# Eight of twelve w_down block sums moved from the projections to the input unit stage, and the down stage's operand loads queued in order of use

## The chip, the cores and the metric

The kernel runs on one NeuronCore of one Trainium2 chip, in one launch. The metric is the device time in microseconds (us); smaller is better. Engines: PE (TensorE, matrix products), DVE (VectorE), ACT (ScalarE), POOL (GpSimd) and SP (SyncE, which here only issues DMA loads). Every engine runs its own instructions in a fixed order; semaphores tie the engines together.

## The reference

One layer of a diffusion backbone over 1024 latent tokens of width 1024, with 256 context tokens. All data are float32.

```python
hx = rmsnorm(x, g_pre_mix) * (1 + sc1) + sh1                # sc, sh, ga: silu(c) @ w_mod + b_mod
u_pool, u_lru, u_gate, g_pool, g_lru = split(hx @ w_in)     # 5 x 1024 columns
y_pool = pool_mixer(u_pool)                                 # window sums, then 4 small products
y_lru  = (h_f + h_b) * gelu(u_gate)                         # two linear scans of gated u_lru
m = sigmoid(g_pool) * (y_pool @ w_proj_pool) + sigmoid(g_lru) * (y_lru @ w_proj_lru)
x = x + ga1 * rmsnorm(m @ w_out)
g, u = split(modulated_rmsnorm(x) @ w_up)                   # 2 x 3072 columns
g = depthwise_conv3x3(g) + b                                # on a 16 x 64 grid
x = x + ga2 * rmsnorm((gelu(g) * u) @ w_down)               # w_down is 3072 x 1024
```

## The kernel before, in words

Each float32 product is made of three products of a rounded high part and a low remainder. `split` makes the two: ACT casts the high part (line 89), DVE subtracts (line 90). `load_w` (lines 92 to 99) loads 512 KB of weights into one of three buffers with the tag "raw" and splits them into one of three "whl" buffers, from which PE multiplies.

The stages, with their place in the span:

- **Preparation** (0 to 80 us): the modulation vectors that the input needs, and normalised tokens hx.
- **Input units** (80 to 280, the pool `z1`): the list `steps` (line 403) names what the program does one after another. `p`, `u`, `g` are units: one `load_w` of w_in and 48 matrix instructions of 128x512 (`unit_mm`, line 243). `a` and `b` are the products after the pooling (`pw`, line 378, stored to yp_d), `c` and `t` prepare the context tokens, and each `m` takes three steps of the generator `mod_steps` (lines 253 to 282).
- **mod_steps** makes two modulation vectors here (j = 0 and 1). For each it loads eight blocks of w_mod (`rawm`) one after another and adds them into `acc` on DVE (lines 265 and 267), sums over the partitions on PE (`pm`, line 271), adds a row of rowv (`rowb`, line 274) and stores the row (line 281). `rawm` and `rowb` use the same three "raw" buffers as `load_w`.
- **LRU** (280 to 590, the pool `z2`): `lru_in(0)` (line 450) begins with a `load_w` of w_in, and its `unit_mm` is the first work of PE in the stage.
- **Projections** (590 to 820, the pool `pj`): first yps, the last gate units and hy; then eight `pp_unit` and eight `pl_unit` (48 matrix instructions each; a pl unit ends with two operations on DVE, lines 603 and 604, and a store of a block of m_d). Among them stand twelve `down_sums` (line 616) and three `form_pair`, and the loads of w_out (`wo`).
- **Output projection** (827 to 940): for each of eight row blocks a load of `st` from m_d, a split into `mH` (lines 718 and 719) and matrix instructions of line 724.
- **Feed-forward** (945 to 1413): 24 features f; the last act of each is a convolution of eight taps on DVE (line 881), a gelu on ACT (line 889), a product on DVE (line 890) and a store to gu_d.
- **Down stage** (1400 to the end): seven products of twelve sets each. `down_set` loads two halves of a set into a ring of three "raw" and five "rw" buffers (lines 908 and 910) and splits it into three "whl" and five "op" buffers; line 971 multiplies. Sets 0 to 2 of the first product are prepared ahead (line 927), set 3 is the first in an "rw" buffer.

A call of `down_sums(p)` loads the blocks p and 12+p of w_down (512 KB each, on SP), makes four additions of 128x512 on DVE (lines 620 to 623) and stores two blocks of 512 KB to sd_d (on POOL's queue). Four of the seven products of the down stage read sd_d, from the third on. In the kernel before these blocks lie in tiles `pc` of the projection pool.

The order of each engine's instructions is set by a scheduler from the program order and priorities; a DMA on SP waits for its buffer to be free, and the DMAs behind it on SP wait as well.

Of the kernel before, what the change touches and what calls it, by code (L numbers as in the profile page):

```python
# [8 lines left out]
F32 = mybir.dt.float32  # L9
# [31 lines left out]
def block_kernel(ctx: ExitStack, tc: tile.TileContext, x, cx, vecs, rowv, icnt, w_mod1, w_mod, w_in, pool_w,  # L41
# [50 lines left out]
    def load_w(src, n=1024, tag="whl", bufs=3, pool=None, raw=None):  # L92
        if raw is None:
            raw = gpool.tile([P, n], F32, name=uid("raw"), tag="raw", bufs=3)
        nc.sync.dma_start(raw, src)
        w = (pool or gpool).tile([P, 2, n], F32R, name=uid("whl"), tag=tag, bufs=bufs)
        with tc.high_priority(offset=WPRI):
            split(w[:, 0, :], w[:, 1, :], raw)
        return w

    n2raw = gpool.tile([P, 4, 512], F32, name="n2raw", tag="n2raw")
    epsc = cpool.tile([P, 1], F32, name="epsc")
# [185 lines left out]
    with tc.tile_pool(name="z1", bufs=1, reuse_waits="tile") as zp:  # L288
# [111 lines left out]
                modulate(hc[0][:, k, :], hc[1][:, k, :], xcT[:, k, :], k, 1)  # L400

        NHO = 2
        steps = "p6 p7 u6 g6 u7 p4 g7 a3 p5 b3 u4 u5 c m t m p2 a2 u2 p3 b2 m u3 m p0 a1 p1 b1 u0 m u1 m a0 b0".split()
        base = {"p": 0, "u": 16, "g": 24}
        order = [base[s_[0]] + int(s_[1:]) for s_ in steps if s_[0] in base]
        wq = pre
# [2 lines left out]
        for s_ in steps:  # L409
            kind, n = s_[0], int(s_[1:] or 0)  # L410
            if kind in base:
                while n_ld < len(order) and len(wq) < 3:
                    wq.append(load_w(w_in[order[n_ld]]))
                    n_ld += 1
            if kind == "p":
                mm = pool_unit(n)
            elif kind == "u":
                mm = ug_unit(n)
            elif kind == "g":
                mm = gate_unit(0, n)  # L420
            elif kind in "ab":
                pool_out(n, "ab".index(kind), mm)
            elif kind == "c":
                ctx_norm()
            elif kind == "t":
                ctx_mod(mm)
            else:
                some(mods, 3)
# [126 lines left out]
    with tc.tile_pool(name="pj", bufs=1, reuse_waits="tile") as zp:  # L555
# [54 lines left out]
        def piece(dt=F32R):  # L610
            n_pc[0] += 1
            i = n_pc[0] % 5
            return zp.tile([P, 2, 512], dt, name=uid("pc"), tag="mq" if i < 2 else f"bc{i - 2}",
                           bufs=NMQ if i < 2 else 1)

        def down_sums(p):
            ru, rg = piece(F32), piece(F32)
            nc.sync.dma_start(ru, w_down[p * P:(p + 1) * P, :].rearrange("p (h c) -> p h c", h=2))
            nc.sync.dma_start(rg, w_down[(NH + p) * P:(NH + p + 1) * P, :].rearrange("p (h c) -> p h c", h=2))
            V.tensor_add(rg[:, 1, :], ru[:, 1, :], rg[:, 1, :])  # L620
            V.tensor_add(ru[:, 1, :], ru[:, 0, :], ru[:, 1, :])
            V.tensor_add(ru[:, 0, :], ru[:, 0, :], rg[:, 1, :])
            V.tensor_add(rg[:, 0, :], rg[:, 0, :], ru[:, 0, :])
            for i, t in enumerate((ru, rg)):
                G.dma_start(sd_d[p, i], t.rearrange("p h c -> p (h c)"))

        def form_pair(f):
            L, R = slice(0, 512), slice(512, 1024)
            ru, rg = [gpool.tile([P, 1024], F32, name=uid("raw"), tag="raw", bufs=3) for _ in range(2)]
# [17 lines left out]
        wo = []  # L647
        for c in range(4):
            pp_unit(c)
            down_sums(c)  # L650
        for c in range(KT):
            m_last = pl_unit(c)
            if c < 2:
                down_sums(4 + c)
            elif c < 2 + NPF:
                form_pair(c - 2)
            else:
                for p in range(2):
                    down_sums(6 + 2 * (c - 2 - NPF) + p)
            if c < 4:  # L660
                pp_unit(c + 4)
            if c >= 4 and c < 6:
                for k in range(4 * c - 16, 4 * c - 12):
                    wo.append(load_w(w_out[k * P:(k + 1) * P, :], tag="big", bufs=8, pool=zp))
# [106 lines left out]
    with tc.tile_pool(name="ff", bufs=1, reuse_waits="tile") as zp:  # L771
# [131 lines left out]
            ("Y", False, lambda p: wlo(1)(p)[:, H1], gul(1, 0), "n4"),  # L903
        ]

        def down_set(q, p, raw, op, raw2=None):
            dst, first, wsrc, gsrc, form = PRODS[q]
            nc.sync.dma_start(raw[:, H0], wsrc(p))
            if gsrc is not None:
                nc.sync.dma_start(raw[:, H1], gsrc(p))  # L910
            if form == "n2":
                nc.sync.dma_start(raw2[:, H0], gul(0, 1)(p))
                nc.sync.dma_start(raw2[:, H1], gul(1, 1)(p))
            with tc.high_priority(offset=DPRI):
                if form == "n2":
                    V.tensor_sub(N[:, 0, p, :], raw[:, H1], raw2[:, H0])
                    V.scalar_tensor_tensor(N[:, 1, p, :], raw2[:, H1], -1.0, N[:, 0, p, :],
                                           op0=ALU.mult, op1=ALU.subtract)
                elif form in ("n3", "n4"):
                    V.tensor_add(raw[:, H1], raw[:, H1], N[:, 1, p, :])  # L920
                if form in ("n1", "n2"):
                    split(op[:, 0, H0], op[:, 1, H0], raw[:, H0])
                    split(op[:, 0, H1], op[:, 1, H1], N[:, int(form[1]) - 1, p, :])
                else:
                    split(op[:, 0, :], op[:, 1, :], raw)
            return op
# [189 lines left out]
```

## Time and profile before

| | |
|---|---|
| median of 3 runs | 1656.9 us (1655.75 to 1661.22) |
| the profiled execution's own time | 1658.86 us |
| its span | 1657.1 us |
| PE busy | 1568.0 us, 95% |
| DVE busy | 1244.5 us, 75% |
| ACT busy | 684.1 us, 41% |
| POOL busy | 163.3 us, 10% |
| DMA | 267.12 MB, mean 161 GB/s |

Times of rows are microseconds from the start of the span. Busy time is time in instructions; a row of an engine in order of time gives in brackets how long the engine was idle before the instruction and what released it. PEclk is the clock that TensorE was granted, as a share of full speed. "To landing" is the time from the issue of a DMA to its completion.

### The profile page before, as it was taken

The page shows a single profiled execution, that of the slowest core. Times are in us where ns is not written, and L with a number is a line of the kernel's source. Part 1 is how long each engine was busy: PE and PEld are TensorE (multiplying, and loading weights), DVE is VectorE, ACT ScalarE, POOL GpSimd, SP SyncE. Part 2 cuts the span into 40 slices and gives each one's busy share as a digit, 9 for nine tenths or more (in the row PEclk, how much of TensorE's full clock was granted, in tenths as well). Part 3 has the DMA queues.
Part 4 walks back from the last instruction along what each step waited for, and adds up shares of the span by engine and source line. Part 5 has one row for each costly group of instructions (what it writes and reads, how often), then busy time and mean ns, then how long its engine had stood idle before and what let it go on. Part 6 is the DMA issues. An engine that isn't in the chain of part 4 may idle for free.

```text
span 1657.1 us, 18358 instructions
## 1 busy us (share of the span) xinstructions
PE 1568.0 (95%) x6976; PEld 1267.1 (76%) x6976; DVE 1244.5 (75%) x1416; ACT 684.1 (41%) x828; POOL 163.3 (10%) x232
## 2 busy tenths in 40 slices
PE   6899999999899999998699889999999999799997
PEld 4588888877778788886488667888888888588886
DVE  7777574787887745565457879999999998677567
ACT  8523322655577643122034333333433333445443
POOL 1300200111112221121110000000000000000000
PEclk9999999999999999999899999999999999899999
DMA  8335354324232277899934432222222222885544
GB/s 311 114 100 172 127 196 141 121 83 152 77 127 89 89 261 286 294 326 339 344 114 165 166 114 76 88 78 78 88 86 80 76 89 102 276 296 201 191 166 165
DMA packets 87990, 267.12 MB, mean 161 GB/s; under 512 B 9719, under 2 KB 9847, under 8 KB 87134
## 3 DMA queue, kind: packets, MB, share of 16 engines
q1 hardware_dynamic: 64382, 183.23, 33.2%
q0 software_dynamic: 23520, 82.73, 13.3%
q8 instruction: 54, 0.88, 0.2%
q14 instruction: 34, 0.28, 0.1%
HBM read 199.32 MB, written 66.60 MB: 160 GB/s over the span
## 4 chain that ended last, share of the span: by engine, by line
PE 29%; DVE 15%; DMA 3%; ACT 2%; issue 1%; DVEq 0%; ACTq 0%
PE pb L971 7%; DVE gc L881 6%; PE pb L724 5%; PE pb L758 5%; PE pd L971 4%; PE pc L971 3%; DMA raw<-in_w_up_dram 3%; PE pc L758 3%; PE pd L758 2%; DVE wf L90 2%; DVE gc L890 1%; DVE whl L90 1%; ACT whl L89 1%; DVE gc L865 1%; DVE raw L811 1%
## 5 line engine op out<-in xcount | busy, mean ns | idle before, releaser
L243 PE MATMUL pu<-hx,whl 128*128 128x512 f32 x1056 | 266.7, 392 | 1.5 <-DVE whl L90 1.3
L881 DVE SCALAR_TENSOR_TENSOR gc<-gc,vec 128x945 f32<-128x945 f32 (+1 forms) x192 | 234.4, 1221 | 7.1 <-ACT gc L870 2.9
L89 ACT CAST whl<-raw 128x1024 fp32r<-128x1024 f32 (+1 forms) x109 | 108.9, 1001 | 294.1 <-PE pu L243 58.8
L243 PEld LDWEIGHTS pu<-hx,whl 128*128 128x128 f32 x1056 | 186.7, 188 | 39.6 <-DVE whl L90 2.0
L90 DVE TENSOR_TENSOR whl<-raw,whl 128x1024 fp32r<-128x1024 f32 (+1 forms) x109 | 127.9, 1178 | 88.7 <-ACT whl L89 88.4
L243 PE MATMUL pg<-hx,whl 128*128 128x512 f32 x480 | 116.0, 394 | 0.0
L243 PEld LDWEIGHTS pg<-hx,whl 128*128 128x128 f32 x480 | 88.9, 189 | 19.1
L243 PE MATMUL pb<-hy,whl 128*128 128x512 f32 x384 | 93.1, 403 | 10.3 <-DVE sgp L603 5.9
L724 PE MATMUL pb<-whl,mH 128*128 128x512 f32 x384 | 91.0, 398 | 11.4 <-ACT mH L718 11.4
L243 PEld LDWEIGHTS pb<-hy,whl 128*128 128x128 f32 x384 | 74.4, 195 | 28.2 <-ACT whl L89 8.0
L758 PE MATMUL pb<-h,wf 128*128 128x512 f32 x384 | 93.0, 391 | 2.1 <-ACT fk L820 2.1
L758 PE MATMUL pb<-h,whl 128*128 128x512 f32 x384 | 94.5, 390 | 0.0
L724 PEld LDWEIGHTS pb<-whl,mH 128*128 128x128 f32 x384 | 73.2, 192 | 27.2 <-ACT mH L718 11.8
L89 ACT CAST wf<-raw 128x1024 fp32r<-128x1024 f32 x42 | 44.2, 1052 | 118.4 <-PE pb L758 53.1
L758 PEld LDWEIGHTS pb<-h,wf 128*128 128x128 f32 x384 | 71.5, 188 | 18.8 <-ACT fk L820 4.2
L758 PEld LDWEIGHTS pb<-h,whl 128*128 128x128 f32 x384 | 71.9, 188 | 15.3 <-ACT fk L820 0.5
L758 PE MATMUL pc<-nf,wf 128*128 128x512 f32 x288 | 73.7, 404 | 8.7 <-ACT nf L778 4.5
L971 PE MATMUL pb<-op 128*128 128x512 f32 x306 | 79.0, 394 | 0.0
L758 PEld LDWEIGHTS pc<-nf,wf 128*128 128x128 f32 x288 | 53.7, 192 | 26.6 <-DVE gc L865 7.6
L499 PE MATMUL pg<-xp,whl 128*128 128x512 f32 x192 | 62.2, 420 | 8.9 <-ACT i L505 8.5
L758 PE MATMUL pc<-nf,w 128*128 128x512 f32 x288 | 69.2, 389 | 0.0
L971 PEld LDWEIGHTS pb<-op 128*128 128x128 f32 x306 | 58.2, 191 | 12.5 <-DVE CA L999 0.3
(310 smaller groups left out, 2952.1 us busy)
## 6 DMA issues: line engine op xcount, KB each, us to landing
raw<-in_w_up_dram SPq DMA_DIRECT2D x51, 512.0 KB, 3.6
raw<-in_w_in_dram SPq DMA_DIRECT2D x40, 512.0 KB, 4.7
rawm<-in_w_mod_dram SPq DMA_DIRECT2D x32, 512.0 KB, 4.1
rw<-gu_d SPq DMA_DIRECT2D x63, 256.0 KB, 4.4
pc<-in_w_down_dram SPq DMA_DIRECT2D x24, 512.0 KB, 5.9
sd_d<-pc POOLq DMA_DIRECT2D x24, 512.0 KB, 6.3
gu_d<-gc POOLq DMA_DIRECT2D x24, 512.0 KB, 2.9
raw<-gu_d SPq DMA_DIRECT2D x33, 256.0 KB, 3.3
```

What stands on the lines that cost most here:

```text
L89: A.copy(hi, src)
L90: V.tensor_sub(lo, src, f32(hi))
L243: mm = T.matmul(ps[:, h * 512:(h + 1) * 512], wv[:, wi, k, :], act(h, k, ai), start=st, stop=sp)
L499: T.matmul(pg[:, h * 512:(h + 1) * 512], wg[:, wi, m, :], xp[:, ai, h * 512:(h + 1) * 512], start=(i == 0), stop=(i == 2))
L724: mm = T.matmul(ps[:, h * 512:(h + 1) * 512], mh[ai][:, k, :], wo[k][:, wi, h * 512:(h + 1) * 512], start=(k == 0 and i == 0), stop=(k == ...
L758: mm = T.matmul(ps, w(wi, j), b(ai, j), start=(start and j == 0 and i == 0), stop=(j == 3 and i == 2), skip_group_check=True)
L811: V.tensor_add(ru[:, L], ru[:, L], rg[:, R])
L865: V.tensor_sub(gc[:, 0, 0:512], v, u2)
L881: V.scalar_tensor_tensor(o, gv[:, r0 + dr:r1 + dr, c0 + dc:c1 + dc], cw(i, j), o, op0=ALU.mult, op1=ALU.add)
L890: V.tensor_mul(gc[:, 1, :], gc[:, 0, :], u)
L971: T.matmul(bank[dst](t), op[:, gi, 512 + t * P:512 + (t + 1) * P], op[:, wi, H0], start=(first and p == 0 and i == 0), stop=(p == NH - 1 a ...
```

## The change

Three things change in the program:

1. `down_sums` becomes a helper that is given its two tiles. Eight of its twelve calls (p = 0 to 7) become the steps `d0` to `d7` of the input unit stage, with two tiles of the tag "raw" each, so they share the three buffers of `load_w` and `mod_steps`.
2. In the projections only four calls (p = 8 to 11, after pp_unit 0 to 3) stay; those after the pl units are gone.
3. Each load of `down_set` is ordered behind the load of the set before it (`issue_after`).

```diff
+    def down_sums(p, tiles):
+        ru, rg = [t if len(t.shape) == 3 else t.rearrange("p (h c) -> p h c", h=2) for t in tiles]
+        nc.sync.dma_start(ru, w_down[p * P:(p + 1) * P, :].rearrange("p (h c) -> p h c", h=2))
...
-        steps = "p6 p7 u6 g6 u7 p4 g7 a3 p5 b3 u4 u5 c m t m p2 a2 u2 p3 b2 m u3 m p0 a1 p1 b1 u0 m u1 m a0 b0".split()
+        steps = "p6 p7 u6 g6 u7 p4 g7 a3 p5 b3 u4 d0 u5 d1 c m t m p2 a2 u2 d2 p3 b2 m u3 d3 m p0 a1 d4 p1 b1 u0 d5 m u1 d6 m a0 b0 d7".split()
...
+            elif kind == "d":
+                down_sums(n, [gpool.tile([P, D], F32, name=uid("raw"), tag="raw", bufs=3) for _ in range(2)])
...
             pp_unit(c)
-            down_sums(c)
+            down_sums(NH - 4 + c, (piece(F32), piece(F32)))
         for c in range(KT):
             m_last = pl_unit(c)
-            if c < 2:
-                down_sums(4 + c)
-            elif c < 2 + NPF:
+            if 2 <= c < 2 + NPF:
                 form_pair(c - 2)
-            else:
-                for p in range(2):
-                    down_sums(6 + 2 * (c - 2 - NPF) + p)
...
+        ld = []
+
         def down_set(q, p, raw, op, raw2=None):
             dst, first, wsrc, gsrc, form = PRODS[q]
-            nc.sync.dma_start(raw[:, H0], wsrc(p))
...
+            with ExitStack() as es:
+                if ld:
+                    es.enter_context(tc.issue_after(ld[-1].ins))
+                ld.append(nc.sync.dma_start(raw[:, H0], wsrc(p)))
+                if gsrc is not None:
+                    ld.append(nc.sync.dma_start(raw[:, H1], gsrc(p)))
```

Line numbers after the change are higher by 11 to 13 in the stages before the projections (line 262 becomes 273, line 271 becomes 282), and by 2 in the down stage.

**SP at the end of the input unit stage.** These are the last loads of the stage, up to the weights of `lru_in(0)` (the last row but one before, the last after). Before:

```order
L262 DMA rawm235_1943<-in_w_mod_dram 128x1024
L262 DMA rawm238_1998<-in_w_mod_dram 128x1024
L262 DMA rawm239_2001<-in_w_mod_dram 128x1024
L256 DMA rowb241_2007<-in_rowv_dram 1x1024
L95 DMA raw254_2078<-in_w_in_dram 128x1024
L95 DMA raw256_2083<-in_lru_w_dram 128x512
```

After:

```order
L273 DMA rawm247_2003<-in_w_mod_dram 128x1024
L103 DMA raw250_2058<-in_w_down_dram 128x1024
L104 DMA raw251_2059<-in_w_down_dram 128x1024
L273 DMA rawm252_2068<-in_w_mod_dram 128x1024
L273 DMA rawm253_2071<-in_w_mod_dram 128x1024
L267 DMA rowb255_2077<-in_rowv_dram 1x1024
L103 DMA raw262_2117<-in_w_down_dram 128x1024
L104 DMA raw263_2118<-in_w_down_dram 128x1024
L95 DMA raw270_2158<-in_w_in_dram 128x1024
```

The loads of the sums d6 (raw250, raw251) and d7 (raw262, raw263) now stand among and behind the last blocks of w_mod and ahead of the weights of `lru_in(0)` (raw270). raw270 takes the buffer of rowb255 and waits until DVE has read that row at line 285.

**DVE at the same place.** The end of the second modulation vector (`acc`), the last pooling outputs (`yp`), and the remainder of the weights of `lru_in(0)`. Before:

```order
L90 TENSOR_TENSOR whl255_2080<-raw254_2078,whl255_2080 128x1024
L342 TENSOR_TENSOR q225_1857<-up224_1854 128x16x64
L384 TENSOR_SCALAR yp228_1867<-pw230_1876,vec_67 128x512
L90 TENSOR_TENSOR pw214_1769<-praw213_1767,pw214_1769 128x512
L90 TENSOR_TENSOR d217_1779<-xa216_1774,d217_1779 128x1024
L349 TENSOR_TENSOR xa226_1859<-q225_1857 128x1024
L351 TENSOR_TENSOR xa226_1859<-xa226_1859,inv212_1765 128x1024
L352 TENSOR_TENSOR xa226_1859<-xa226_1859,up224_1854 128x1024
L90 TENSOR_TENSOR d227_1864<-xa226_1859,d227_1864 128x1024
L274 TENSOR_TENSOR acc204_1698<-pm240_2004,rowb241_2007 1x1024
L384 TENSOR_SCALAR yp242_2011<-pw244_2020,vec_67 128x512
```

After:

```order
L278 SCALAR_TENSOR_TENSOR acc212_1738<-rawm252_2068,cs_89,acc212_1738 128x1024
L395 TENSOR_SCALAR yp256_2081<-pw258_2090,vec_67 128x512
L278 SCALAR_TENSOR_TENSOR acc212_1738<-rawm253_2071,cs_89,acc212_1738 128x1024
L395 TENSOR_SCALAR yp259_2099<-pw261_2108,vec_67 128x512
L285 TENSOR_TENSOR acc212_1738<-pm254_2074,rowb255_2077 1x1024
L105 TENSOR_TENSOR raw263_2118<-raw262_2117,raw263_2118 128x512
L106 TENSOR_TENSOR raw262_2117<-raw262_2117 128x512
L107 TENSOR_TENSOR raw262_2117<-raw262_2117,raw263_2118 128x512
L108 TENSOR_TENSOR raw263_2118<-raw263_2118,raw262_2117 128x512
L90 TENSOR_TENSOR whl271_2160<-raw270_2158,whl271_2160 128x1024
```

Before, the weights of `lru_in(0)` (whl255) were split nine operations ahead of the addition of `pm`. Now that addition stands behind the last pooling outputs, and the weights (whl271) are split after it. On PE the two instructions of `pm` stand directly before the first of `lru_in(0)`; before, the 24 of the last pooling product stood between.

**SP at the start of the down stage.** Sets 0 to 2 are in raw1016 to raw1020; the set 3 is rw1022, the first one that is loaded into an "rw" buffer. Before:

```order
L910 DMA raw1020_9415<-gu_d_6509 128x512
L908 DMA raw1032_9558<-in_w_down_dram 128x512
L910 DMA raw1032_9558<-gu_d_6509 128x512
L908 DMA raw1034_9576<-in_w_down_dram 128x512
...
L908 DMA raw1052_9742<-in_w_down_dram 128x512
L910 DMA raw1052_9742<-gu_d_6509 128x512
L908 DMA rw1022_9426<-in_w_down_dram 128x512
```

After:

```order
L912 DMA raw1020_9415<-gu_d_6509 128x512
L910 DMA rw1022_9426<-in_w_down_dram 128x512
L912 DMA rw1022_9426<-gu_d_6509 128x512
L982 DMA ga_9435<-row_d_82 128x1024
L910 DMA rw1024_9486<-in_w_down_dram 128x512
```

The loads of six later sets (raw1032 to raw1052, two loads each) no longer stand ahead of the loads of set 3.

## Rows read from the trace of the kernel before

**Rows 1.** stretches of the span: PE, PEld, DVE, ACT, POOL busy, PEclk, DMA share, GB/s

```profile
80.00:280.00 200.00, 199.68 (x880) 163.23 (x879) 132.14 (x126) 56.08 (x69) 20.52 (x47) 1.00 0.43 140
...
590.00:760.00 170.00, 170.00 (x752) 140.76 (x751) 85.07 (x97) 50.43 (x56) 28.47 (x50) 1.00 0.88 311
...
820.00:830.00 10.00, 2.48 (x6) 1.99 (x7) 2.46 (x3) 0.95 (x1) 2.00 (x2) 0.50 0.45 158
...
740.00:812.00 72.00, 61.71 (x251) 49.05 (x250) 44.17 (x53) 14.53 (x16) 10.72 (x19) 0.93 0.96 349
```

**Rows 2.** PE in order of time, 740 to 860: start, length, line, operation, idle before

```profile
756.90 11.04 PE L243 MATMUL pb<-hy,whl 128*128 128x512 f32 x48
772.07 2.07 PE L243 MATMUL pb<-hy,whl 128*128 128x512 f32 x4 [4.13 <-ACT whl L89]
...
789.15 11.33 PE L243 MATMUL pb<-hy,whl 128*128 128x512 f32 x48 [3.01 <-DVE sgp L603]
803.39 12.77 PE L243 MATMUL pb<-hy,whl 128*128 128x512 f32 x48 [2.90 <-DVE sgp L603]
827.52 32.83 PE L724 MATMUL pb<-whl,mH 128*128 128x512 f32 x133 [11.37 <-ACT mH L718]
```

**Rows 3.** DMA issues of 590 to 830: count, KB each, median us to landing

```profile
pc<-in_w_down_dram SPq DMA_DIRECT2D x24, 512.0 KB, 5.9
sd_d<-pc POOLq DMA_DIRECT2D x24, 512.0 KB, 6.3
...
m_d<-sgp POOLq DMA_DIRECT2D x7, 512.0 KB, 7.2
...
st<-m_d POOLq DMA_DIRECT2D x2, 448.0 KB, 5.1
```

**Rows 4.** line 620, first of a sum's four additions: shortest/median/longest ns

```profile
L620 DVE TENSOR_TENSOR pc<-pc,pc x12: 681/692/695, 653.3 to 807.8; 128x512 f32<-128x512 f32 x12
```

**Rows 5.** DMA issues of 100 to 290: count, KB each, median us to landing

```profile
rawm<-in_w_mod_dram SPq DMA_DIRECT2D x19, 512.0 KB, 4.3
raw<-in_w_in_dram SPq DMA_DIRECT2D x12, 512.0 KB, 6.0
yp_d<-yp POOLq DMA_DIRECT2D x8, 512.0 KB, 3.8
```

**Rows 6.** DVE in order of time, around the two vector additions

```profile
215.07 1.21 DVE L274 TENSOR_TENSOR acc<-pm,rowb 1x1024 f32<-1x1024 f32 x1
...
274.31 1.21 DVE L274 TENSOR_TENSOR acc<-pm,rowb 1x1024 f32<-1x1024 f32 x1 [13.05 <-PE pm L271]
...
281.82 1.28 DVE L267 SCALAR_TENSOR_TENSOR acc<-rawm,cs,acc 128x1024 f32<-128x1024 f32 x1
```

**Rows 7.** PE in order of time, end of the input unit stage

```profile
272.40 1.88 PE L271 MATMUL pm<-acc,ones 128*128 128x512 f32 x4
...
279.69 0.62 PE L243 MATMUL pu<-hx,whl 128*128 128x512 f32 x2
```

**Rows 8.** ACT in order of time, start of the down stage

```profile
1421.96 1.06 ACT L889 ACTIVATE gc<-gc 128x1024 f32<-128x1024 f32 x1 [7.74 <-DVE gc L881]
1422.92 1.03 ACT L89 CAST op<-rw 128x1024 fp32r<-128x1024 f32 x1
```

**Rows 9.** PE in order of time, start of the down stage

```profile
1406.59 1.07 PE L971 MATMUL pb<-whl 128*128 128x512 f32 x4
...
1424.00 0.80 PE L971 MATMUL pd<-op 128*128 128x512 f32 x1 [10.90 <-ACT op L89]
```

**Rows 10.** SP in order of time, start of the down stage

```profile
1415.68 0.33 SPq L908 DMA_DIRECT2D raw<-in_w_down_dram  x1
...
1416.53 0.43 SPq L908 DMA_DIRECT2D rw<-in_w_down_dram  x1
```

**Rows 11.** DVE in order of time, start of the down stage

```profile
1408.79 1.20 DVE L881 SCALAR_TENSOR_TENSOR gc<-gc,vec 128x945 f32<-128x945 f32 x1 [1.31 <-ACT gc L870]
...
1415.56 6.30 DVE L881 SCALAR_TENSOR_TENSOR gc<-gc,vec 128x1008 f32<-128x1008 f32 x5
```

More of the change, by code (lines that the diff above doesn't have):

```diff
@@ L99, in load_w @@
         return w
+    def down_sums(p, tiles):
+        ru, rg = [t if len(t.shape) == 3 else t.rearrange("p (h c) -> p h c", h=2) for t in tiles]
+        nc.sync.dma_start(ru, w_down[p * P:(p + 1) * P, :].rearrange("p (h c) -> p h c", h=2))
+        nc.sync.dma_start(rg, w_down[(NH + p) * P:(NH + p + 1) * P, :].rearrange("p (h c) -> p h c", h=2))
+        V.tensor_add(rg[:, 1, :], ru[:, 1, :], rg[:, 1, :])
+        V.tensor_add(ru[:, 1, :], ru[:, 0, :], ru[:, 1, :])
+        V.tensor_add(ru[:, 0, :], ru[:, 0, :], rg[:, 1, :])
+        V.tensor_add(rg[:, 0, :], rg[:, 0, :], ru[:, 0, :])
+        for i, t in enumerate((ru, rg)):
+            G.dma_start(sd_d[p, i], t.rearrange("p h c -> p (h c)"))
     n2raw = gpool.tile([P, 4, 512], F32, name="n2raw", tag="n2raw")
@@ L614, in piece @@
                            bufs=NMQ if i < 2 else 1)
[L616 to L625, printed above, removed]
         def form_pair(f):
@@ L904, in block_kernel @@
         ]
+        ld = []
         def down_set(q, p, raw, op, raw2=None):
             dst, first, wsrc, gsrc, form = PRODS[q]
-            nc.sync.dma_start(raw[:, H0], wsrc(p))
[L909 to L913, printed above, removed]
+            with ExitStack() as es:
[4 more added lines that the diff above has]
+                    ld.append(nc.sync.dma_start(raw[:, H1], gsrc(p)))
+                if form == "n2":
+                    ld.append(nc.sync.dma_start(raw2[:, H0], gul(0, 1)(p)))
+                    ld.append(nc.sync.dma_start(raw2[:, H1], gul(1, 1)(p)))
             with tc.high_priority(offset=DPRI):
```

## The prediction

> **What bounds the kernel now.** The profiled execution took 1658.86 us, with a span of 1657.1; the sum below is made against 1658.86, and the median of the runs shown, 1656.9, lies 0.1% under it. I began with the table of busy shares: PE is busy for 95% of the span, so a microsecond is won only where PE idles, and any work put in PE's way is paid in full. Then I read the stretches of the span [rows 1]. From 80 to 280, where eight sums are to go, PE idles for 0.3 us in 200; DVE has 68 us free, and the DMA engines are at 0.43 with 140 GB/s. From 590 to 760 PE never idles either, though the DMA share is 0.88. From 740 to 812 the share is 0.96 with 349 GB/s, and there PE does fall idle. The instructions of PE in order of time [rows 2] show it: four pl units, with waits of 4.13, 3.01 and 2.90 us between them, for weights and for the PSUM bank that DVE's line 603 frees, then 11.37 us until the output projection gets its mH. All of these releasers stand at the end of transfers that take long: a store of m_d takes 7.2 us and a load of w_down 5.9 [rows 3].
>
> **Term 1, the projections: -26 us.** Eight sums leave: 16 loads and 16 stores of 512 KB, and 32 additions. Line 620 runs twelve times between 653.3 and 807.8 [rows 4]. Two of the sums that go stand behind the first two pl units, six behind the last three, so that most of the 16.8 MB goes out of the stretch that moves 72 us times 349 GB/s, 25 MB. What is left there are the loads of w_out and pl weights, sg_d and one form_pair. I therefore let the four pl units run back to back: from 756.90, four times 11.04 less the overlap of 0.1, to about 800.5. The output projection needs a load of st from m_d, which waits for the store of pl unit 6. That unit would end at 789.6; two DVE operations of 1.2 us, a store, a load of 5.1 [rows 3] and ACT's copy follow. For the store I take 4.5 us, between 7.2 with the traffic of now and 3.8, a store at 140 GB/s [rows 5]. That makes 803 instead of 827.52, a gain of 24.5 us. After the long idle time PE also ran slow: its granted clock was 0.50 from 820 to 830 [rows 1], 1.2 of 2.4 GHz, and 133 instructions took 32.83 us where 133 x 0.23 (11.04 / 48) make 30.6. These 2.2 us go too if PE idles for only 2.5 us; I count 1.5, which makes 26. Bounds: 19 if the 4.13 us for weights stay and the store still takes 7.2; 28 if the store takes 3.8 and nothing waits. The additions save nothing, since DVE is not what PE waits for in a free pipeline.
>
> **Term 2, the input unit stage: +16 us.** Two prices seem small. The 8 x 4 additions of 0.69 us [rows 4] are 22 us of DVE, which has 68 free. The transfers add 16.8 MB in 200 us, 84 GB/s to 140. Units take their weights from the ring some 20 us ahead, so single late loads are covered. What is not covered is the ring itself. A buffer that held weights is free when DVE has split them; one that held a sum is free only when its store has landed. All loads on SP stand in one order behind whichever waits. The modulation vector j = 1 takes eight blocks through this ring one after another, and now d3 to d6 stand between them.
>
> I followed the chain through the new order by each load's buffer. It starts where the first vector's addition is done, now at 216.3 [rows 6]; with 1.3 us that DVE's extra work costs there, the second load of d3 goes out at 217.6. Then, one after another: its load, the sum, its store, a block of w_mod, the load of d4, the sum, its store, three blocks of w_mod, a load of d6, its sum, and the last block. These are eight loads, each 4.3 us to landing [rows 5] plus about 0.1 until the next instruction, 35.2; two stores at 3.7 (3.8 in [rows 5]), 7.4; six additions to acc at 1.28 [rows 6], 7.7; and three sums with what DVE does between their additions, 5.1 + 7.9 + 2.4 = 15.4 (2.8 each if nothing stood between). With 0.9 for queueing that gives 284.2, and pm (1.88 us, [rows 7]) ends at about 286.2. Before, pm was done at 274.3, in front of the last pooling product, and nobody waited for it.
>
> Now somebody does. The weights of lru_in(0) take the buffer of the row that is added to pm. After pm come that addition, 1.25; the load, 4.4; ACT's cast, 1.05 (near 1.03 in [rows 8]); with gaps of 0.2 PE begins lru_in(0) at 293.1 instead of 279.69 [rows 7]: 13.4 us. PE idles in it twice, some 5 and 7 us, and begins slow; from [rows 1, 2] that was 2.2 us after 11.4 idle, here I take 2.6 for the two. Sum 16. Behind it I see no slack that would take it back: the LRU stage opens with exactly this unit. **Bounds.** The lower one is a chain that is hidden by the work in front: pm still stands last on PE, at 279.7, and then 6.8 us for addition, load and cast follow, 8 with the queueing. The upper bound is a chain whose loads and stores go as in the projections, 5.9 and 6.3 [rows 3]: 8 x 1.5 + 2 x 2.6 more, 33. The stage's traffic would be nearer to 140 than to 311 GB/s, and in this chain one or two transfers run at a time, so I stay at its own rows.
>
> The trace's row for such a load is 4.3 us [rows 5]. The Trainium skill, page "DMA: Bandwidth & Descriptors", section "Anatomy of one DMA — SWDGE (gpsimd) path", gives a fit of 2.0 us plus the bytes over 436 GB/s for a DMA issued from GpSimd, 3.2 us for 512 KB as an estimate; by it the eight loads would be 9 us shorter, the chain would all but vanish behind the work in front, and the time would be that of the first rival. The trace does not agree with it for these loads, which SP issues.
>
> **Term 3, the down stage's start: -3 us.** PE ends its last prepared set at 1413.1 and starts the next at 1424.00, idle for 10.90 us until ACT has cast it [rows 9]. Its load was issued at 1416.53, after those of six later sets, the last at 1415.68 [rows 10]. Moved ahead, it can go when its buffer is free, after the last feature's products at about 1406.6 [rows 9], up to 9.7 us earlier. But ACT casts it at 1422.92 behind the gelu at 1421.96 [rows 8], which waits for the convolution. DVE's first tap is at 1408.79, and three splits of later sets stand between its taps; the last five, with none between, take 6.30 [rows 11]. Eight in a row end at 1408.8 + 8 x 1.26 = 1418.9, the gelu at 1420.0, the cast at 1421.0. So 3 us; bounds 0, if the taps stay where they are, and 9.7.
>
> **Sum.** -26 + 16 - 3 = -13: 1658.86 - 13 = 1645.9; taken down by the 0.1%, 1645.
>
> **The rivals.**
> *The vector chain is hidden.* If the loads land some 1 us faster or DVE slips the sums in between, only the wait behind pm is left, 8 us: 1658.9 - 26 + 8 - 3 = 1638. For it: DVE and DMA have room [rows 1]; against it: eight loads in a row at the median of today already overrun. Chance 0.17.
> *The projections keep their last wait.* If the stall before the output projection is one of latency (store, then load, then cast) more than of traffic, 11.4 us stay and only the 10.3 between the units and 2 more go, -12 to -14: 1659 - 13 + 16 - 3 = 1659, no change. For it: the store cannot begin before its unit ends. Against it: that unit ends 14 us earlier relative to PE's need once the others are not late. Chance 0.15.
> *Slower: the ring's round trips cost as much as in the projections.* Loads at 5.9 and stores at 6.3 in the chain give the upper bound of 33, and 33 - 26 - 3 = +4 to +7, with a clock that stays low a little longer: 1663 to 1666. This decides as soon as term 2 exceeds 29, which needs loads above 5.5 us in the chain. For it: the stage's loads of w_in take 6.0 us even now [rows 5], where several are out at once. Chance 0.16.
> *The reordered loads change nothing or collide with the last stores of gu_d*: 1648 and inside the forecast's range, 0.05.
>
> **How the numbers follow.** The forecast, 1645 with its own bounds of 1638 to 1651, has 0.47. About 0.3%, 5 us, is what a measurement of this kernel can tell from no change. Faster by more than that (below 1652): the forecast, the first rival and the fourth, 0.69, less a little where the terms lie at their bad ends, 0.67. Same (1652 to 1662): most of the second rival and the bad ends, 0.17. Slower: the third, 0.16. The range 1632 to 1663 takes in the hidden chain with the best end of terms 1 and 3, and the low part of the slower case.
>
> **What would show it.** Right: PE without waits over 1 us between the pl units, and the output projection within 3 us of the last of them; pm at 284 to 286 as the last thing ahead of lru_in(0), which starts 11 to 16 us later, released by ACT's cast; the granted clock low right after it; the fourth set of the down stage about 3 us sooner after the last feature. Wrong: pm ahead of the last pooling product's end; lru_in(0) less than 9 or more than 25 us later; units of the input stage waiting for weights; or an output projection that still waits for over 8 us.

## The result, and the profile after

The changed kernel took 1665.62 us, median of ten runs (1662.75 to 1670.51); the kernel before, over ten runs, 1657.10 (1655.75 to 1661.22). The ratio is 1.0051, 95% interval 1.0040 to 1.0063: slower by half a per cent, where 1645 was forecast and 1632 to 1663 was the range. The profiled execution took 1662.75 us with a span of 1661.0, against 1658.86 and 1657.1; it is the fastest of the ten, so the trace accounts for 3.9 us of a difference of 8.5 between the medians.

Stretches of the span after the change (columns as in [rows 1]):

```profile
80.00:280.00 200.00, 195.85 (x859) 160.42 (x858) 140.43 (x143) 54.33 (x65) 27.23 (x56) 0.99 0.54 186
280.00:300.00 20.00, 8.12 (x17) 3.88 (x15) 8.87 (x11) 0.69 (x1) 3.16 (x6) 0.74 0.76 274
300.00:320.00 20.00, 16.70 (x76) 14.07 (x77) 8.26 (x10) 3.89 (x5) 1.09 (x2) 0.83 0.79 278
590.00:610.00 20.00, 17.62 (x67) 14.37 (x68) 12.52 (x9) 8.35 (x7) 5.22 (x3) 0.82 0.18 66
740.00:812.00 72.00, 72.00 (x319) 59.64 (x318) 38.20 (x41) 20.35 (x24) 8.12 (x13) 1.00 0.86 289
```

Of these [rows 1] has the first and the last: PE idled 0.3 us from 80 to 280 before, now 4.2; from 740 to 812 it idled 10.3, now not at all. The new holes are from 280 to 320, where PE is busy for 24.8 of 40 us at a granted clock of 0.74 and 0.83 of full speed, and from 590 to 610.

PE in order of time, at the end of the input unit stage, answers to [rows 7]; the last row is the first instruction of `lru_in(0)`:

```profile
288.05 2.93 PE L389 MATMUL pw<-d,pw 128*128 128x512 f32 x6 [6.53 <-DVE yp L395]
293.51 3.68 PE L282 MATMUL pm<-acc,ones 128*128 128x512 f32 x4 [2.54 <-DVE acc L278]
303.30 1.22 PE L254 MATMUL pu<-hx,whl 128*128 128x512 f32 x2 [6.10 <-ACT whl L89]
```

The first unit of the LRU stage starts at 303.30 instead of 279.69, 23.6 us late. By the end of the stage's last gate unit it is 25.2 (584.35 against 559.12). Then the way from the LRU stage to the projections. Before, in order of time:

```profile
548.04 11.08 PE L243 MATMUL pg<-hx,whl 128*128 128x512 f32 x48
560.91 22.08 PE L243 MATMUL pb<-hx,whl 128*128 128x512 f32 x96 [1.79 <-ACT i L505]
```

After:

```profile
573.27 11.08 PE L254 MATMUL pg<-hx,whl 128*128 128x512 f32 x48
592.38 24.41 PE L254 MATMUL pb<-hx,whl 128*128 128x512 f32 x96 [8.02 <-ACT sg L478]
```

The wait in front of the first unit of the projections has grown from 1.79 to 8.02 us, and that unit and the next, together, take 24.41 us instead of 22.08, at a clock of 0.82 in the stretch above. The lag is now 33.8 us. It is given back in the projections. These rows answer to [rows 2]: the last pp unit, the four pl units as one group of 192 instructions without any wait, and the output projection:

```profile
779.83 11.04 PE L254 MATMUL pd<-yps,whl 128*128 128x512 f32 x48
790.71 43.68 PE L254 MATMUL pb<-hy,whl 128*128 128x512 f32 x192
836.48 33.36 PE L721 MATMUL pb<-whl,mH 128*128 128x512 f32 x144 [2.09 <-ACT mH L715]
```

PE reaches the output projection at 836.48 instead of 827.52: the lag fell by 24.85 us, to 8.96, and by another 2.0 to 6.99 within the next three row blocks (870.47 against 863.48 for the fourth), where the clock no longer drops. At the start of the down stage, the counterpart to [rows 9], the wait fell from 10.90 to 7.87 us:

```profile
1418.31 1.52 PE L973 MATMUL pb<-whl 128*128 128x512 f32 x6
1427.70 0.80 PE L973 MATMUL pd<-op 128*128 128x512 f32 x1 [7.87 <-ACT op L89]
```

What the profiled execution shows is so: +33.8 before the pl units, -26.8 in the projections and behind them, -3.0 at the down stage: +4.0 for a span that is 3.9 longer.

### The profile page after: what moved, and what is told of

Same layout as the page of the kernel before. It is cut to its first block, busy times and chain, and to the rows that moved or that the text cites. A ratio compares the mean times of both kernels' runs of the same rounds, so it can differ in the third digit from the quotient of the medians.

```text
span 1661.0 us, 18380 instructions
## 1 busy us (share of the span) xinstructions
PE 1571.9 (95%) x6976; PEld 1270.6 (76%) x6976; DVE 1246.0 (75%) x1416; ACT 684.9 (41%) x828; POOL 165.9 (10%) x232
## 4 chain that ended last, share of the span: by engine, by line
PE 30%; DVE 14%; DMA 3%; ACT 2%; issue 1%; DVEq 0%; ACTq 0%
PE pb L973 7%; DVE gc L878 6%; PE pb L755 6%; PE pb L721 5%; PE pd L973 4%; PE pc L755 3%; PE pc L973 3%; DMA raw<-in_w_up_dram 3%; PE pd L755 3%; DVE wf L90 2%; DVE gc L887 1%; ACT whl L89 1%; DVE whl L90 1%; DVE gc L862 1%; DVE raw L808 1%
## 5 line engine op out<-in xcount | busy, mean ns | idle before, releaser
L254 PE MATMUL pb<-hy,whl 128*128 128x512 f32 x384 | 87.9, 389 | 0.0
```

What stands on the lines that cost most here:

```text
L254: mm = T.matmul(ps[:, h * 512:(h + 1) * 512], wv[:, wi, k, :], act(h, k, ai), start=st, stop=sp)
```

## The experiments

The theory after the trace was: the move costs what the shared ring of raw buffers costs in the input unit stage (25 us with the slow clock) plus a PSUM bank at the way to the projections (8 us); the projections and the down stage win what was forecast. The main rival: the added traffic and the additions on DVE cost the time, whichever buffer they use. Times are medians on chips on which the kernel before took 1659.7 to 1661.4, so the ratio is what to compare; "on the scale of 1657" below means the ratio times 1657.

**The order of the down stage's loads alone** (the third part of the change put into the kernel before).

```diff
+        ld = []
         def down_set(q, p, raw, op, raw2=None):
...
+                if ld:
+                    es.enter_context(tc.issue_after(ld[-1].ins))
...
```

> The kernel before with only the down stage's loads queued in order of use; nothing else changes. Theory (ring and bank): this part is worth the 3 us that the changed kernel's trace shows at the start of the down stage, so about 1654 us against 1657, with PE idle for some 8 us instead of 10.9 before the fourth set. Rival (the parts are not independent, and the order pays only where the stages before it moved): no change, 1657, or slower.

Ratio 0.998 (0.9971 to 0.9988): 3.3 us faster. PE's wait for the fourth set is again 7.87 us:

```profile
1422.81 0.80 PE L976 MATMUL pd<-op 128*128 128x512 f32 x1 [7.87 <-ACT op L89]
```

The load of that set is issued at 1405.91 in this kernel, 10.6 us earlier than in [rows 10], and 3 us come of it: the gelu on ACT stands in front of the cast, as the prediction had it.

**The eight early sums left out.** They are made nowhere; the down stage reads the four remaining blocks in their place, as many bytes.

```diff
-                down_sums(n, [gpool.tile(...) for _ in range(2)])
+                pass
...
-            ("X", False, lambda p: sd_d[p, 1, :, H1], None, "n1"),
+            ("X", False, lambda p: sd_d[8 + p % 4, 1, :, H1], None, "n1"),
```

> The changed kernel with the eight early block sums left out altogether (the down stage reads the four blocks that are still made, in place of the others, so its loads are as many). Theory: the projections then win what the changed kernel's trace shows there, 27 us, and the down stage 3, with nothing paid for it: 1627 us. Rival (the changed kernel's gain in the projections is only the other side of its late start): 1640 or more, with a wait of about 10 us left before the output projection.

Ratio 0.9817 (0.9804 to 0.983): 30.3 us faster. The output projection starts at 802.32, after a wait of 0.94 us:

```profile
802.32 33.34 PE L721 MATMUL pb<-whl,mH 128*128 128x512 f32 x144 [0.94 <-ACT mH L715]
```

So the gain forecast for the projections and the down stage, 29, is there in full, and the eight early sums cost 38.8 us together (2.34% between this kernel and the changed one).

**The sums in a buffer pair of their own**, a tile that nothing else uses before the output projection.

```diff
-                down_sums(n, [gpool.tile([P, D], F32, name=uid("raw"), tag="raw", bufs=3) for _ in range(2)])
+                down_sums(n, [n2raw[:, 0:2, :], n2raw[:, 2:4, :]])
```

> The changed kernel, but the eight early sums use a buffer pair of their own (the tile n2raw, which nothing else needs before the output projection) in place of the shared raw ring; as many loads, additions and stores in the same stage. Theory (the loss in the input unit stage is the shared ring, where loads of weights and of w_mod wait for stores of sums): most of the 25 us goes, the first unit of the LRU stage starts within 5 us of where it started before, and the time is 1627 to 1634 us. Rival (the loss is the added traffic and the 22 us of additions on DVE, whatever the buffer): the start stays 15 to 25 us late, 1645 to 1660 us.

Ratio 0.9896 (0.9878 to 0.9913): 17.2 us faster than the kernel before, 25.7 better than the changed one, and yet outside what either side expected: the first unit of the LRU stage is 11.9 us late, neither within 5 nor 15 to 25. The wait at the modulation vector was gone, but PE now waited at another place, for the context rows `xs`:

```profile
181.61 1.94 PE L155 MATMUL pt<-ident,xs 128*128 128x128 f32 x8 [9.98 <-DVE xs L148]
...
291.61 0.62 PE L254 MATMUL pu<-hx,whl 128*128 128x512 f32 x2
```

SP in order of time shows one step of it. The second load of the fifth sum waited until 153.30 for the pair, and the load of the context rows, which the kernel before issues at 147.07, went out behind it:

```profile
148.29 0.33 SPq L103 DMA_DIRECT2D n2raw<-in_w_down_dram  x1
153.30 0.33 SPq L104 DMA_DIRECT2D n2raw<-in_w_down_dram  x1
...
154.21 0.37 SPq L144 DMA_DIRECT2D xs<-in_cx_dram  x1
```

It is not the only step: from 171.44 to the scaling of the rows at 180.71 DVE is busy without a gap, and three additions of a sum are among what it does there. How much of the 9.98 us is SP's order and how much DVE's is not separated. The profiled execution is also the slowest of this kernel's six, 8.3 us above their median.

Nor does this kernel show what the pair by itself does for the modulation vector: with the buffer free earlier, the scheduler also moved the sums forward. Their first load goes out at 46.03 and their last at 216.41, so that none stands among the blocks of the second vector, where the changed kernel has the loads of five sums (215.14 to 293.40).

**The first PSUM tile of the projections in another bank pair.** In the built programs the last gate unit's tile lies in the second pair of banks before and in the first after the change, and the first tile of the projections lies in the first pair in both. No row names a bank, but the releasers of the wait below agree. One more line makes it the second pair.

```diff
+        pbank("c")
         for j, (which, c) in enumerate(gq):
```

> The changed kernel with one line more that makes the projections' first PSUM tile lie in the other bank pair, the one that the LRU stage frees first; the order of work is the same. Theory (6 us of the loss is PE waiting for a PSUM bank at the handover from the LRU stage, 8 with the slow clock after it): that wait falls from 8.0 us to about 2 and the time by 6 to 8, to 1658 us. Rival (the wait there only mirrors how late ACT is at that place, whichever bank): the wait stays near 8 us and the time at 1665.

Ratio 0.9999 (0.9989 to 1.0009), 8.6 us less than the changed kernel, and the wait is back at 1.79, for another releaser:

```profile
587.05 23.64 PE L254 MATMUL pb<-hx,whl 128*128 128x512 f32 x96 [1.79 <-ACT i L518]
```

On ACT, in the changed kernel, one sees why the bank matters. The tanh `sg` that frees the first pair stands behind the last scan's operations; the tile in the other pair is free after the `i` of line 518, at 586.07, 6.3 us earlier:

```profile
584.96 1.11 ACT L518 ACTIVATE i<-pg,vec 128x1024 f32<-128x1024 f32 x1 [0.74 <-DVE i L547]
...
591.32 1.01 ACT L478 ACTIVATE sg<-pg 128x1024 f32<-128x1024 f32 x1
```

The two traces show 7.0 of the 8.6 us at this place: 6.2 less of waiting and 0.8 less for the two units (23.64 for 24.41). They do not come back to the 22.08 of the kernel before: the granted clock was 0.83 from 587 to 597, where it was 1.00 from 560 to 570 before, behind the same wait of 1.79 us. Why was not tried.

**The sums added in the ring, but not stored** (the down stage again reads other blocks).

```diff
-        for i, t in enumerate((ru, rg)):
+        for i, t in enumerate((ru, rg) if p >= 8 else ()):
```

> The changed kernel with the eight early sums loaded and added in the shared raw ring, but not stored (the down stage reads four other blocks in their place). A buffer is then free when DVE has added, as it is after weights, and a quarter of the stage's new traffic is gone... half of it, the stores. Theory (of the 24 us at the first unit of the LRU stage about half is waiting for stores to land before a load may take the buffer, the rest is the chain of loads itself and the wait behind the modulation vector): that unit starts 9 to 14 us late in place of 24, and the time is 1637 to 1643 against 1657. Rival (the stores do not matter; loads and additions alone delay it): 20 us or more late, 1648 or above. Other rival (it is the stores alone): less than 5 us late, 1632 or below.

Ratio 0.988 (0.9847 to 0.9914), 19.9 us faster than before, 1640.17 us as measured, within what the theory had given. The first unit of the LRU stage is only 6.8 us late, less than the 9 to 14 expected:

```profile
286.52 0.73 PE L254 MATMUL pu<-hx,whl 128*128 128x512 f32 x2 [1.34 <-ACT whl L89]
```

Of 23.6 us at this unit some 17 go with the stores, so that the loads and additions alone explain a third at most. What the stores hold is the buffer; it is not their traffic. From 216 to 290 as many bytes moved per second without them (the first row below, columns as in [rows 1]; the second is the changed kernel), and a load of w_down landed no sooner there, in 4.0 us against 3.5. (The bank at the way to the projections is the early one in this program, so nothing was lost there.)

```profile
216.00:290.00 74.00, 70.84 (x308) 57.11 (x308) 53.18 (x59) 14.69 (x17) 6.07 (x12) 1.00 0.67 220
216.00:290.00 74.00, 67.47 (x290) 54.71 (x290) 46.99 (x51) 14.04 (x17) 9.25 (x18) 0.98 0.66 224
```

**The own pair, with the loads ordered behind weight loads.** This was to take away the wait for the context rows.

```diff
+            if after is not None:       # after: the last DMA that load_w issued, lw[-1]
+                es.enter_context(tc.issue_after(after.ins))
...
-                down_sums(n, [gpool.tile(...) for _ in range(2)])
+                down_sums(n, [n2raw[:, 0:2, :], n2raw[:, 2:4, :]], lw[-1])
...
-        steps = "... u4 d0 u5 d1 c m t m p2 a2 u2 d2 ..."
+        steps = "... u4 u5 c m t m p2 d0 a2 u2 d1 p3 b2 d2 m u3 d3 m p0 d4 a1 p1 d5 b1 u0 d6 m u1 d7 m a0 b0"
```

> As the kernel with the sums in their own buffer pair, but each sum's loads ordered on SP behind a weight load, so that the first sums no longer stand ahead of the loads of the context rows. Theory (what that kernel still lost, 10 us, was PE waiting for the context rows, whose load stood on SP behind a load that waited for the sums' buffer): the wait goes and the time is 1627 to 1633. Rival (the remaining loss is traffic and DVE's additions and shows up at another place): 1637 to 1645 as before.

Ratio 0.9978 (0.9963 to 0.9993): a clear miss, 3.6 us faster than before instead of 24 to 30. In front of the context transposes PE now waited 2.12 us, for ACT and not for the rows. The second vector was better off too: `pm` ran at 278.45 instead of 293.51, though the loads of four sums go out from 241.16 on. But eight sums, packed into the rest of the stage and with one pair of buffers, were late at its end, and DVE's order passed this on. DVE in order of time: an addition of a sum waits 8.47 us for its load, and behind it stand the vector addition and the pooling output `yp`:

```profile
287.55 0.69 DVE L110 TENSOR_TENSOR n2raw<-n2raw 128x512 f32<-128x512 f32 x1 [8.47 <-DMA n2raw<-in_w_down_dram]
...
290.33 1.21 DVE L290 TENSOR_TENSOR acc<-pm,rowb 1x1024 f32<-1x1024 f32 x1
291.47 0.73 DVE L400 TENSOR_SCALAR yp<-pw,vec 128x512 f32<-128x512 f32 x1
```

and PE waits for just that `yp`:

```profile
292.25 2.93 PE L394 MATMUL pw<-d,pw 128*128 128x512 f32 x6 [7.74 <-DVE yp L400]
...
317.01 9.28 PE L259 MATMUL pu<-hx,whl 128*128 128x512 f32 x30 [6.54 <-ACT whl L89]
```

The second row is a later wait, 6.54 us for weights of the LRU stage. The last sum's addition waited 9.16 us for its load shortly before, at 305.13; a link between the two was not followed up.

So a buffer of one's own is not the whole matter. An operation that waits for a late load holds up what is queued behind it on its own engine, on SP as on DVE.

**The own pair, with the loads on POOL's queue.**

```diff
+        ld = G if p < 8 else nc.sync
...
-        nc.sync.dma_start(ru, w_down...)
+        ld.dma_start(ru, w_down...)
...
```

> As the kernel with the sums in their own buffer pair, but their loads issued on POOL's queue, so that on SP nothing waits for the sums' buffer. Theory (the remaining loss there was SP's order): PE's wait for the context rows goes, 1627 to 1634, unless stores of POOL that wait behind those loads hold up a buffer of the stage, up to 5 us more. Rival (traffic or DVE): the first unit of the LRU stage stays 10 us late, 1640.

Ratio 0.9954 (0.9937 to 0.997), a miss too. The scheduler put the first of these loads into the preparation, which moved 265 GB/s in 80 us where it moved 218, and the first input unit was 11.8 us late (the row below stood at 63.50):

```profile
75.30 0.96 PE L248 MATMUL pu<-hx,whl 128*128 128x512 f32 x3 [0.76 <-DVE hx L164]
```

And PE still waited for the context rows:

```profile
194.66 1.94 PE L156 MATMUL pt<-ident,xs 128*128 128x128 f32 x8 [11.29 <-DVE xs L149]
```

The second of these rows' loads takes a buffer of `yp`, and SP waited 7.8 us until the store of `yp` had landed. POOL issues that store, but no load on its queue held it up here: it went out some 0.5 us after DVE had written `yp` (at 167.49, for 0.75 us).

```profile
168.79 0.54 POOL L397 DMA_DIRECT2D yp_d<-yp  x1 [2.63 <-DVE yp L396]
```

So the part of the theory that named SP's queue was too narrow: with no load of an early sum on SP the wait is still there. What makes the rows late in this kernel stays open.

**The sums in the LRU stage**, one in each of its eight loops, in their own pair, each ordered behind the loop's weight load.

```diff
...
             nxt = lru_in(c + 1) if c + 1 < KT else None
+            down_sums(c, [n2raw[:, 0:2, :], n2raw[:, 2:4, :]], lw[-1])
```

> The eight sums one by one in the loop of the LRU stage, in their own buffer pair, each ordered on SP behind the loop's weight load; nothing of them in the input unit stage. Theory (a sum costs nothing where its buffer is its own and its loads hold up no load that is due): 1627 to 1634. Rival (DVE is on the path in the LRU stage, where PE waits for its chain, so 2.8 us of additions in each of eight loops show up in part): 1638 to 1650.

1622.75 us, ratio 0.978 (0.9754 to 0.9806): 2.2% faster than the kernel before, 2.7% than the changed one, the best here, and better than the 1627 to 1634 expected. In the LRU stage DVE is now busy for 266.4 of 310 us where it was 240.5, the DMA share is 0.51 instead of 0.34, and PE is busy for 4 us more, not less:

```profile
280.00:590.00 310.00, 301.75 (x1412) 244.75 (x1411) 266.40 (x232) 183.76 (x179) 65.33 (x53) 0.99 0.51 172
```

The output projection starts at 795.31:

```profile
795.31 33.35 PE L727 MATMUL pb<-whl,mH 128*128 128x512 f32 x144 [0.96 <-ACT mH L721]
```

In the two traces that is 7 us earlier than without the sums at all. A wait of PE in the LRU stage for ACT's `i`, 3.87 us at 387.66 in the kernel without early sums, does not occur in this one, and the clock stays up there (1.00 from 350 to 400, 0.97 in the other). Why the additions' places on DVE have this effect was not tried. It is a gift of the order, and no one should count on it.

**Only the first three early sums, and only the last five**, in the shared ring, the others left out (the down stage reads other blocks).

```diff
-                down_sums(n, [gpool.tile(...) for _ in range(2)])
+                if n < 3:            # the other kernel: n >= 3
+                    down_sums(n, [gpool.tile(...) for _ in range(2)])
```

> The changed kernel with only the first three early sums (d0 to d2) made, in the shared raw ring; d3 to d7 are left out (the down stage reads other blocks in their place). Theory (the first three cost only the 4.8 us by which the changed kernel was late at 212 us; the rest of the loss comes from the sums that stand between the blocks of the second modulation vector): the first unit of the LRU stage starts 4 to 6 us late and the time is 1634 to 1637 on a scale where the kernel before takes 1657 and the one without early sums 1627 to 1630. Rival (each sum costs alike, 3 us): 9 us late, 1638 to 1641.

> The changed kernel with only the last five early sums (d3 to d7), in the shared raw ring; d0 to d2 are left out. Theory: the first unit of the LRU stage starts about 19 us late (24 less the 4.8 of the first three), and the PSUM bank at the handover is again the one that is freed late, since the order of the last units is that of the changed kernel, 8 us more: 1652 to 1659. Rival (each sum costs alike): 15 us late at that unit. Other rival (the late bank belongs to all eight): no wait over 2 us at the handover, 1645 to 1650.

The first three: ratio 0.9877 (0.986 to 0.9893), 9.9 us above the kernel without early sums. On the scale of 1657 that is 1636.6, within the expected 1634 to 1637, but the first unit of the LRU stage is 8.4 us late, where 4 to 6 were expected and the rival, 3 us for each sum, had 9. Most of it is one wait in the context transposes, here longer than in the changed kernel:

```profile
178.85 1.12 PE L155 MATMUL pt<-ident,xs 128*128 128x128 f32 x4 [6.50 <-DVE xcT L157]
...
288.14 0.62 PE L254 MATMUL pu<-hx,whl 128*128 128x512 f32 x2
```

The last five: ratio 0.9997 (0.9985 to 1.001), 29.8 us above the kernel without early sums, as expected. The three waits at the end of the stage are those of the changed kernel, `lru_in(0)` starts 19.6 us late, and at the way to the projections PE waits 8.02 us again:

```profile
282.73 2.93 PE L389 MATMUL pw<-d,pw 128*128 128x512 f32 x6 [5.96 <-DVE yp L395]
289.54 3.75 PE L282 MATMUL pm<-acc,ones 128*128 128x512 f32 x4 [3.88 <-DVE acc L278]
299.28 1.22 PE L254 MATMUL pu<-hx,whl 128*128 128x512 f32 x2 [5.99 <-ACT whl L89]
```

9.9 and 29.8 make 39.7 where all eight cost 38.8: in the time the parts add up, though at the first unit 8.4 and 19.6 us make 28.0 where all eight give 23.6. For the last five an equal price, 15 us at that unit, is out. But if the bank costs 8.6 us here too, the last five are left with 4.2 us each, against 3.3 for the first three, so that most of the difference between the two groups is the bank.

## Why the prediction was wrong

**Term 1, the projections, -26: right.** 24.85 and 2.0 us make 26.8; the forecast was 24.5 and 1.5. The kernel without early sums shows the same by itself. PE still waits 2.09 us for the output projection's first operand, 2.5 were expected. The rival in which the projections keep their last wait is out.

**Term 3, the down stage, -3: right**, 10.90 to 7.87, alone and within the change, and by the step that was named.

**Term 2, the input unit stage, +16: wrong, 33.8 in the profiled execution and 38.8 by the ratios**, both with the bank that the term does not name. The mechanism was named rightly: a buffer is free only when a store has landed, loads wait in order, the second vector comes late, and the weights of `lru_in(0)` wait behind `pm`. Four sizes fail.

First, its start: "with 1.3 us that DVE's extra work costs there". PE waited 3.83 us for the copies of the context transposes, which stand on DVE behind accumulations that wait for their blocks:

```profile
176.39 0.66 PE L155 MATMUL pt<-ident,xs 128*128 128x128 f32 x4 [3.83 <-DVE xcT L157]
```

The second load of d3 went out at 221.06 instead of 217.6. Second, the chain. On DVE, after the change, the last addition of d3, a block of w_mod, the last addition of d4, a block, the first and the last addition of d6, a block, the pooling output and the last block:

```profile
230.65 0.69 DVE L108 TENSOR_TENSOR raw<-raw,raw 128x512 f32<-128x512 f32 x1
...
240.27 1.28 DVE L278 SCALAR_TENSOR_TENSOR acc<-rawm,cs,acc 128x1024 f32<-128x1024 f32 x1 [4.77 <-DMA rawm<-in_w_mod_dram]
...
252.27 0.69 DVE L108 TENSOR_TENSOR raw<-raw,raw 128x512 f32<-128x512 f32 x1
...
264.94 1.28 DVE L278 SCALAR_TENSOR_TENSOR acc<-rawm,cs,acc 128x1024 f32<-128x1024 f32 x1 [5.72 <-DMA rawm<-in_w_mod_dram]
...
283.26 0.69 DVE L105 TENSOR_TENSOR raw<-raw,raw 128x512 f32<-128x512 f32 x1 [6.66 <-DMA raw<-in_w_down_dram]
...
285.44 0.69 DVE L108 TENSOR_TENSOR raw<-raw,raw 128x512 f32<-128x512 f32 x1
286.05 1.28 DVE L278 SCALAR_TENSOR_TENSOR acc<-rawm,cs,acc 128x1024 f32<-128x1024 f32 x1
287.24 0.75 DVE L395 TENSOR_SCALAR yp<-pw,vec 128x512 f32<-128x512 f32 x1
292.08 1.28 DVE L278 SCALAR_TENSOR_TENSOR acc<-rawm,cs,acc 128x1024 f32<-128x1024 f32 x1 [4.09 <-DMA rawm<-in_w_mod_dram]
```

By the forecast's own terms d3 ends at 227.1, the block behind it at 236.5, d4 at 248.9, the next block at 258.5, d6 at 277.4, and the last block starts at 283.1. It came to 231.3, 241.6, 253.0, 266.2, 286.1 and 292.1. Seen from its late start the chain ran 0.6 to 1.6 us over plan up to d4; the block behind d4's store cost 3.6 more, and at the end it was 5.7 over. The transfers from 216 to 294 were not slow in the median:

```profile
raw<-in_w_down_dram SPq DMA_DIRECT2D x9, 512.0 KB, 3.5
rawm<-in_w_mod_dram SPq DMA_DIRECT2D x8, 512.0 KB, 4.6
sd_d<-raw POOLq DMA_DIRECT2D x8, 512.0 KB, 4.7
```

A load of w_down landed in 3.5 us, below the 4.3 that the sum took, a block of w_mod in 4.6 and a store in 4.7, above the 3.7. Third, the pooling output at 287.24 stands behind the additions of d6, for whose load DVE waited 6.66 us: PE waited 6.53 us for that output, with the last quarter of the pooling product behind it. The forecast let that product run ahead of the chain; it hid nothing. It adds nothing to the sum below either, since `pm` waited 2.54 us more for the last block. Fourth, `pm` ran at the low clock, 3.68 us for 1.88 ([rows 7]). 3.5 + 5.7 + 1.8, less 0.8 for a way from `pm` to the first unit that was a little shorter (6.1 us for 6.9), are the 10.2 us between the forecast 13.4 and the measured 23.6. The slow clock behind it was priced at 2.6; between the first unit's start and the end of the stage 1.6 were lost net.

The Trainium skill, page "DMA: Bandwidth & Descriptors", section "Anatomy of one DMA — SWDGE (gpsimd) path", has a fit for DMAs issued from GpSimd that gave an estimate of 3.2 us for these 512 KB. The trace's 3.5 for w_down loads on SP lies nearer to it than the 4.3 of [rows 5] does, the 4.6 for blocks of w_mod farther off; by the fit the chain should have been hidden, and it was not. By the medians above its eight loads and two stores make 42.9 of the 71.0 us from 221.06 to 292.08; the rest is additions, what stands between them on DVE, and waits.

The Trainium skill says in the same section of that page that DMA engines do not wait on semaphores and that any wait happens on the issuing sequencer before dispatch. The rows of SP in the kernel with the own buffer pair agree with this: the load of the context rows went out 7.1 us later than before, behind a load that waited.

**The step that was missing.** "Behind it I see no slack that would take it back: the LRU stage opens with exactly this unit." No slack was there, but a new wait was: the bank at the way to the projections, 6.2 us of waiting and 2.3 of slow clock behind it; 8.6 by the medians of the experiment, whose trace still has 1.6 of the slow clock. The order of the rows of PE around `pm` had been read for its waits, and not for what it does to the two PSUM tiles that pm and the units of the LRU stage share in turn. The wait's releaser shows the exchange: it is `sg` with all eight sums and with the five last alone, and `i` with the first three, without the stores and in all kernels with the own pair. In the two kernels with `sg`, `pm` runs behind the last pooling product; in those with `i`, ahead of its end (but for the one in which a line sets the bank).

**The rivals.** The slower one, "the ring's round trips cost as much as in the projections", gave 1663 to 1666 and a chance of 0.16, and the time came out there. But its mechanism did not: loads stayed at 3.5 to 4.6 us, far from 5.9. A right time for the wrong reason. Its condition, a term 2 above 29, held. The hidden chain is out by the 23.6 us, and the reordered loads without effect by the 3 us of the down stage.

**What the prediction's own signs say.** None of its signs of being wrong came: `pm` stood last, no unit of the input stage waited for weights, the output projection waited 2.09 us, and the 23.6 us lie between the 16 of its signs of being right and the 25 of those of being wrong. The signs had no place for a second loss behind the first unit. One sum of the range is also off: the hidden chain with the best ends of terms 1 and 3 (8, 28 and 9.7) gives 1629, which 1632 does not take in; nothing in the result turns on it.

What stays open: why the ten runs of the changed kernel spread over 7.8 us and its median lies 2.9 above the profiled one, and in which stage; there is one trace for it. The kernel with its own pair spreads more, 1639.08 to 1650.49, with its profiled execution the slowest.

## What to carry to other kernels

Work that is moved into a stage where every engine has room is not free if it enters a ring of buffers or an in-order queue on which due work stands: look at what is queued behind each of its waits, here on SP and on DVE, before adding up busy shares. Place it where its buffer is its own and where its loads are issued with time to spare, and look for the stage in which nothing behind it is due: the same eight sums cost 39 us in one stage and less than nothing in the next. And when a move changes the order on PE, compare which PSUM buffer each hand-over now waits for.

## What the runs showed that was not expected

The same order of work with one PSUM tile in another bank pair is 8.6 us faster (ratios 1.0051 and 0.9999), and no row of busy time tells of it: only the releaser of one wait changes, from `sg` to `i`. And a stage with 26 us more of DVE work and a DMA share of 0.51 instead of 0.34 ran its PE work earlier, not later.
